# Sixteen blocks of 256 rows in place of interleaved rows, in a DMA-only ifftshift

## The chip, the cores and the metric

The kernel runs on one core of a Trainium2 chip. The metric is the time of one execution on the device in microseconds (us), as the median of several runs; lower is better. Besides the plain runs there is one profiled execution, whose trace records every instruction and every DMA packet.

## The reference

```python
def setup_inputs():
    return {"x": np.random.randn(8192, 8192).astype(np.float32)}

def reference(x):
    return np.fft.ifftshift(x)
```

With even sizes this swaps the four quadrants of the matrix: `out[r, c] = x[(r + 4096) % 8192, (c + 4096) % 8192]`. Nothing is computed; 268 MB are read and 268 MB written. A row of float32 has 32 KB, half a row 16 KB, and each half row of the output is one contiguous half row of the input.

## The kernel before

The kernel has no tile in on-chip memory and no compute instruction of its own. It is a list of DMAs that copy from the input to the output in the chip's main memory (HBM). Two instruction queues issue them in turn: SP's (`nc.sync`) writes the left half of the output rows (`h = 0`), from the right half of the input, and ACT's (`nc.scalar`) writes the right half (`h = hc`), from the left half of the input. In the profile SP's DMA queue is q1 and ACT's q10.

Each DMA is described by three dimensions, outermost first, as pairs of a step in elements and a count (line 26):

```python
dims = [[C, ENGINES], [ENGINES * C, per], [1, hc]]
```

The innermost is a contiguous half row of 16 KB. The outermost has 16 entries, one for each of the core's 16 DMA engines; here its step is one row (C = 8192 elements, 32 KB). The middle one has `per` = 32 entries with a step of 16 rows. So engine e copies the rows e, e + 16, e + 32 and so on of a group of 512 rows, and at any time the 16 engines work on neighbouring rows. A group's half is 8 MB. The loop of line 27 goes over the 16 groups; in each, line 29 takes SP's half and ACT's half. `src_row` (line 28) is the group's first row in the input.

There are 32 DMAs in all, 16 on each queue. The framework gives each one of eight semaphores in turn, four for each queue; before a semaphore is used again, the queue's issuing instruction waits for the DMA that had it, the one four before on that queue. Nothing else orders the DMAs. At the end SP waits until all have landed. The profile puts every DMA issue at line 30.

Of the kernel before, what the change touches and what calls it, by code (L numbers as in the profile page):

```python
# [1 line left out]

# [4 lines left out]


ENGINES = 16


@with_exitstack
def kernel(
    ctx: ExitStack,
    tc: tile.TileContext,
    x: bass.AP,
    out: bass.AP,
):
    nc = tc.nc
    R, C = x.shape  # L20
    hr = R // 2
    hc = C // 2


    per = 32
    dims = [[C, ENGINES], [ENGINES * C, per], [1, hc]]
    for row in range(0, R, ENGINES * per):
        src_row = (row + hr) % R
        for queue, h in ((nc.sync, 0), (nc.scalar, hc)):
            queue.dma_start(  # L30
                out=bass.AP(out.tensor, out.offset + row * C + h, dims),
                in_=bass.AP(x.tensor, x.offset + src_row * C + hc - h, dims),
            )


# [1 line left out]
_INS = ['x']  # L37
_OUTS = [((8192, 8192), 'float32')]


def kernel(**inputs):
    import numpy as _np
    import concourse.bacc as _bacc
    import concourse.tile as _tile
    from concourse import mybir as _mybir
    from concourse.bass_utils import run_bass_kernel_spmd as _run

    nc = _bacc.Bacc("TRN2", target_bir_lowering=False, num_devices=1)  # L48
    arrays, args = {}, []
    for name in _INS:  # L50
        a = _np.ascontiguousarray(inputs[name])
        if a.dtype.kind in "iu":
            a = a.astype(_np.int64)
        arrays[f"in_{name}_dram"] = a
        args.append(nc.dram_tensor(f"in_{name}_dram", a.shape, _mybir.dt.from_np(a.dtype), kind="ExternalInput").ap())
    for i, (shape, dtype) in enumerate(_OUTS):
        dt = _mybir.dt.from_np(_np.dtype(dtype))
        args.append(nc.dram_tensor(f"out_{i}_dram", shape, dt, kind="ExternalOutput").ap())
    with _tile.TileContext(nc) as tc:
        kernel(tc, *args)  # L60
    r = _run(nc, [arrays], core_ids=[0])
    got = tuple(r.results[0][f"out_{i}_dram"] for i in range(len(_OUTS)))
    return got[0]
```

## Time and profile before

| | us |
|---|---|
| median of 3 runs | 822.56 |
| lowest and highest | 821.65, 823.45 |
| the profiled execution | 822.98 |
| span of that execution, first to last instruction | 821.2 |
| from issue to landing of a DMA, median, ACT's queue | 204.1 |
| the same, SP's queue | 204.0 |

The profile's page shows the span in 40 equal slices of 20.5 us, with the mean busy share of the 16 DMA engines in tenths (9 is 90% or more) and the bytes that they moved, in GB/s; each byte copied is counted once there, though it is read and written. By the page, memory traffic in both directions together is 654 GB/s over the span. Below that, each DMA queue has its packets, its bytes and the time of its packets as a share of what 16 engines have. A packet here is one half row, or one small write to a semaphore at the end of a DMA's share on an engine. The only compute-engine instructions are four small fills of constants by the GpSimd engine, 0.2 us at the very start.

### The profile page before, as it was taken

The page shows a single profiled execution, that of the slowest core. Times are in us where ns is not written, and L with a number is a line of the kernel's source. Part 1 is how long each engine was busy: PE and PEld are TensorE (multiplying, and loading weights), DVE is VectorE, ACT ScalarE, POOL GpSimd, SP SyncE. Part 2 cuts the span into 40 slices and gives each one's busy share as a digit, 9 for nine tenths or more (in the row PEclk, how much of TensorE's full clock was granted, in tenths as well). Part 3 has the DMA queues.
Part 4 walks back from the last instruction along what each step waited for, and adds up shares of the span by engine and source line. Part 5 has one row for each costly group of instructions (what it writes and reads, how often), then busy time and mean ns, then how long its engine had stood idle before and what let it go on. Part 6 is the DMA issues. An engine that isn't in the chain of part 4 may idle for free. (4 is left out here: it accounts for less than half of the span.)

```text
span 821.2 us, 77 instructions
## 1 busy us (share of the span) xinstructions
POOL 0.2 (0%) x4
## 2 busy tenths in 40 slices
POOL 0000000000000000000000000000000000000000
DMA  8999999999999999999999999999999999999998
GB/s 296 333 324 329 331 328 334 330 330 329 327 330 329 331 326 332 332 327 328 330 330 330 330 323 330 324 330 330 332 326 329 330 322 333 329 329 327 330 329 276
DMA packets 16896, 268.44 MB, mean 327 GB/s; under 512 B 512, under 2 KB 512, under 8 KB 512
## 3 DMA queue, kind: packets, MB, share of 16 engines
q1 hardware_dynamic: 8448, 134.22, 50.2%
q10 hardware_dynamic: 8448, 134.22, 49.0%
HBM read 268.44 MB, written 268.44 MB: 654 GB/s over the span
## 5 line engine op out<-in xcount | busy, mean ns | idle before, releaser
L48 POOL MEMSET const-bfloat16-1.0<- 128x1 bf16 x1 | 0.1, 102 | 0.0
L48 POOL MEMSET const-uint8-127<- 128x1 uint8 x1 | 0.1, 102 | 0.0
L48 POOL MEMSET const-float32-0.0<- 128x1 f32 x1 | 0.1, 99 | 0.2 <-issue 0.2
L48 POOL MEMSET const-float32-1.0<- 128x1 f32 x1 | 0.1, 99 | 0.0
## 6 DMA issues: line engine op xcount, KB each, us to landing
out_dram<-in_x_dram ACTq DMA_DIRECT2D x16, 8192.0 KB, 204.1
out_dram<-in_x_dram SPq DMA_DIRECT2D x16, 8192.0 KB, 204.0
```

The source lines that it names most:

```text
L48: nc = _bacc.Bacc("TRN2", target_bir_lowering=False, num_devices=1)
```

## The change

The copy is cut into two halves of the output (rows 0 to 4095 and 4096 to 8191). In each half, an engine gets 256 neighbouring rows: the outermost step becomes `pitch` = 256 rows, 8 MB, and the middle step one row. Each half is copied in four parts of 64 rows an engine. A DMA has now 16 x 64 half rows, 16 MB, and there are 16 DMAs in all, 8 on each queue. SP and ACT keep their halves of the columns, and the issues still alternate. The last four lines are for pitches that leave rows over; with 256 none are left (16 x 256 = 4096) and they issue nothing.

```diff
-    per = 32
-    dims = [[C, ENGINES], [ENGINES * C, per], [1, hc]]
-    for row in range(0, R, ENGINES * per):
+    pitch = 256
+    parts = [64, 64, 64, 64]
+
+    def copy(queue, h, row, pitch, step, n):
+        dims = [[pitch * C, ENGINES], [step * C, n], [1, hc]]
         src_row = (row + hr) % R
-        for queue, h in ((nc.sync, 0), (nc.scalar, hc)):
-            queue.dma_start(
-                out=bass.AP(out.tensor, out.offset + row * C + h, dims),
-                in_=bass.AP(x.tensor, x.offset + src_row * C + hc - h, dims),
-            )
+        queue.dma_start(
+            out=bass.AP(out.tensor, out.offset + row * C + h, dims),
+            in_=bass.AP(x.tensor, x.offset + src_row * C + hc - h, dims),
+        )
+
+    for base in (0, hr):
+        row = base
+        for n in parts:
+            copy(nc.sync, 0, row, pitch, 1, n)
+            copy(nc.scalar, hc, row, pitch, 1, n)
+            row += n
+        rest = base + ENGINES * pitch
+        if rest < base + hr:
+            copy(nc.sync, 0, rest, 1, 1, 1)
+            copy(nc.scalar, hc, rest, 1, 1, 1)
```

## The prediction

> **What bounds the kernel now.** I read the page's slices first, then its queue table, then stretches of the start, then the waits of the issuing queue, and last the trace's single packet records.
>
> ```profile
> span 821.2 us, 77 instructions
> ...
> DMA  8999999999999999999999999999999999999998
> GB/s 296 333 324 329 331 328 334 330 330 329 327 330 329 331 326 332 332 327 328 330 330 330 330 323 330 324 330 330 332 326 329 330 322 333 329 329 327 330 329 276
> DMA packets 16896, 268.44 MB, mean 327 GB/s; under 512 B 512, under 2 KB 512, under 8 KB 512
> ## 3 DMA queue, kind: packets, MB, share of 16 engines
> q1 hardware_dynamic: 8448, 134.22, 50.2%
> q10 hardware_dynamic: 8448, 134.22, 49.0%
> ```
>
> No compute engine matters: the sixteen DMA engines are busy from end to end, at one flat rate. 16,384 packets carry a half row of 16 KB each (the other 512 are the small semaphore writes), so each engine carries 1,024. The mean packet follows: (0.502 + 0.490) x 821.2 us x 16 / 16,384 = 0.795 us, and the packet records give 795 ns too. 1,024 x 0.795 = 814.2 us; the 7.0 us left of the span are the head before the first packet (2.2 us), the last landing with the closing barrier (about 1.2 us after the last packet), and semaphore writes and small gaps. Around the span lie another 1.8 us (822.98 measured for this execution); the median of the runs is 0.4 us below that execution. So **the time is 1,024 times the mean packet**, plus 9.
>
> The mean hides two kinds of packet. By the records 32% take 608 to 611 ns, a hard floor (an engine at 26.8 GB/s), and the others spread up to 1,421 ns at the 99th percentile. A rate that every engine shared equally would put no packet at the floor; these look like chance collisions. The start shows what collides:
>
> ```profile
> 2.20:3.40 1.20, 0.00 (x0) 1.00 1.03 273
> 3.40:5.10 1.70, 0.00 (x0) 1.00 1.01 414
> 5.10:10.00 4.90, 0.00 (x0) 1.00 1.03 348
> 10.00:100.00 90.00, 0.00 (x0) 1.00 1.00 328
> ```
>
> The columns are the stretch, its length, the busy time of POOL, the clock, the DMA share and GB/s. From 2.2 us only SP's queue (q1) has packets; its first sixteen, which all begin within 0.6 us, average 1,090 ns, and the next 48 average 642 ns, almost the floor. At 5.1 us ACT's queue (q10) joins, and within 5 us the rate is 328 and stays there. Sixteen engines on sixteen neighbouring rows of one queue hardly disturb one another; engines on one queue disturb those on the other.
>
> ```profile
> SPq L30 <- DMA out_dram<-in_x_dram: 134.4, 12, 51.3
> ```
>
> These are SP's twelve waits for an earlier DMA to land before it reuses that DMA's semaphore. They cost nothing now: the three issues before already lie in the engines' queues (a DMA takes a median 204 us from issue to landing, four times the 51 us in which one passes).
>
> **The change, part by part.** *Work kept:* the same 16,384 half rows, 1,024 an engine, on the same two queues: no byte is added. *Instructions:* 32 DMAs become 16 of twice the size. That removes 256 semaphore writes, sixteen an engine, at 9 ns by the records: -0.14 us. The issues fall with them; they are hidden behind full queues except the first. It takes 0.65 us now by the trace's instruction record for 32 rows an engine; if the time goes with the rows, 64 rows take 1.3 us and everything begins 0.65 us later; if not, 0. I take 0.65. *Waits:* each queue still waits for its DMA four before; what is behind such a wait is only the next issue on that queue. Now the fourth issue takes 44 us, the first three 0.6 us each, so an engine's queue accepts 96 rows but not 128; with 64 a DMA the second issue will be the long one. Cover: at least 96 rows in each of two queues, 96 x 2 x 0.795 = 153 us. I cost it at 0; if the cover were gone, each wait would show about one first-round packet, 1.1 us, eight times in all, 9 us.
>
> *The order of addresses* is the real change. Now engine e is on row 16k + e: at any moment the sixteen engines of one queue are 32 KB apart, within 512 KB, and each hops 512 KB from packet to packet. Afterwards they are 8 MB apart, all at the same place inside their blocks, on the read and on the write side, and each goes forward by 32 KB. The trace has no row with that spacing, so the price is bounded. Best: every packet at the floor, 1,024 x (0.611 - 0.795) = -188 us. Worst: every packet like the 99th percentile, 1,024 x (1.421 - 0.795) = +641 us; the first round, in which all engines start at the same moment, is not far below (1,090 ns, +302 us). Between these I price collisions. Alone on one queue a packet costs 642 - 611 = 31 ns over the floor against 15 others, 2.1 ns each. With two queues about 7 of the others are on the packet's own queue and 8 on the other: 184 ns = 7 x 2.1 + 8 x p, p = 21 ns. What spares the own queue is, as I read it, the order: neighbouring rows at distinct places of memory. At 8 MB apart nothing spares them if memory folds 8 MB steps onto the same place, and all 15 others cost 21 ns: 611 + 15 x 21.2 = 929 ns. That is +134 ns a packet, +137 us. I take this value; half and double of the added 134 ns give 862 and 1,063 ns.
>
> The rule that speaks against the change: the Trainium skill, "DMA: Bandwidth & Descriptors", section "Latency and other measured facts", reports copies of 16 KiB pieces whose rate per direction falls with the row pitch, 207 GB/s at 512 KiB, 164 at 2 MiB, 103 at 4 and 8 MiB, and 214 with the pitch padded by 4 KiB. By its ratio of 214 to 103 the time here would be some 1,710 us, an estimate from that page. Its copies keep every stream of a tile inside the same 16 KiB window, while here each engine walks on through its whole block, so I don't take that figure; nothing in this trace shows the pitch.
>
> *Sum* on the profiled execution: 822.98 - 0.14 + 0.65 + 137 = 960.5, and 960 on the median's scale.
>
> **The rivals.**
>
> *Kept in step (slower by much).* All engines start together, and the arrivals of a DMA's sixteen semaphore writes lie 1.2 us apart for the first ACT DMA and only 2.5 us for the last of its kind at the end, so something holds the engines within three packets of one another. If that also holds them at the same place of sixteen folded blocks, every packet pays as in the worst rows: 1,024 x 1.09 to 1.421 us + 9.3, that is 1,125 to 1,464 us, and more is not excluded. Against: a packet that gets ahead finds memory free and should run away from the crowd. It decides from a mean packet over 1.09 us.
>
> *Steady streams (faster, the other side).* Engines spread out inside their blocks until each has its own place, and because all then move forward at one speed they stay clear of each other; an engine's two queues are then in the same few rows too, rather than several 512 KB hops apart. For it: 414 GB/s with one orderly queue, so memory can do it. Against: that order needs a spacing that nothing imposes, and the two queues remain. With all of the other queue's disturbance gone, 1,024 x 0.642 + 9.3 = 667 us; with half, (795 + 642) / 2 = 718 ns, 745 us. It decides as soon as the mean packet is below 795 ns.
>
> *A common limit (no change).* The flat 322 to 334 GB/s in 38 of 40 slices could be the total that memory gives for reads and writes mixed, whatever the order; then 823 us, within about 1%. Against: the 32% of packets at the floor, and 414 GB/s before 5.1 us.
>
> *The change doesn't do what it says.* No row names the engine of a packet; if the rows of a DMA were dealt out otherwise than block by block, an engine would hop over blocks. The small spread of landings fits equal shares either way. I fold this into the others.
>
> **How the numbers follow.** Collisions with all others: 0.44, 960 us, its own range 890 to 1,100 (1,024 x 0.862 and 1.063, + 9.3). Kept in step: 0.20, from 1,125 up. Steady streams: 0.26, 667 to 815. Common limit: 0.10, of which 0.04 within 0.2% of the median, 0.04 slower and 0.02 faster; about 0.2% is what a measurement of this kernel can tell from no change. Slower is 0.44 + 0.20 + 0.04 = 0.68, faster 0.26 + 0.02 = 0.28. The low end is 745 us, where half of the cross-queue cost is gone: about 0.10 lies below. The high end is 1,470, the 99th-percentile row kept throughout: about 0.08 lies above. The range is wide because the one cost that counts has no row of its own.
>
> **What would show it.** The mean packet, read from the queue table as above: 929 ns for the forecast, over 1,090 for kept in step, below 795 for steady streams. The stretch just after the first packets, while SP's queue is alone, tests the spacing by itself: now it is 414 GB/s; if 8 MB steps fold together it must be far lower, near 16 x 16 KB / 0.93 us = 282 GB/s or less, and if it is again about 414 my step is wrong, for then the own queue is still spared. If the rate starts low and rises over the first slices, the engines are escaping from the crowd. A spread of a DMA's landings well over 2.5 us would show that they have drifted apart. If SP's waits now leave gaps in the DMA's busy share, the cover was not what I took it for. The forecast is wrong in sign if the early stretch is slow but the later slices exceed 330 GB/s.

## The result: 2.12 times the time

The changed kernel takes 1,761 us (median of 4 runs, 1,733 to 1,794); the kernel before 823.0 us beside it. The ratio is 2.122, 95% interval 2.109 to 2.135. The forecast was slower, but 960 us, and the range ended at 1,470. The slow layouts vary by a few per cent from run to run, so the ratio takes the changed kernel's two runs within 1.5% of its fastest (1,733 and 1,757 us), and below its fastest run is given, as for every kernel that ran only twice; the others have their median.

The page of the profiled execution of the changed kernel (1,733.13 us), with the same lines as shown of before:

```profile
span 1731.3 us, 61 instructions
...
DMA  8999999999899999999989999999998999999999
GB/s 148 157 154 161 148 152 154 156 160 154 148 163 155 154 154 155 163 154 159 153 152 157 155 160 159 159 155 158 153 152 155 151 158 158 154 160 158 154 159 133
DMA packets 16640, 268.44 MB, mean 155 GB/s; under 512 B 256, under 2 KB 256, under 8 KB 256
## 3 DMA queue, kind: packets, MB, share of 16 engines
q1 hardware_dynamic: 8320, 134.22, 49.6%
q10 hardware_dynamic: 8320, 134.22, 49.0%
```

The DMA engines are as busy as before, at less than half the rate. The packets are the same 16,384 half rows, with 256 semaphore writes in place of 512. Each packet takes longer: (0.496 + 0.490) x 1,731.3 x 16 / 16,384 = 1.667 us, where it was 0.795, for the same 16 KB that the fastest packets of both traces move in 0.61. So a busy engine is here for the most part one that waits. The first stretches, the same as shown of before (stretch, length, POOL's busy time, clock, DMA share, GB/s):

```profile
2.20:3.40 1.20, 0.00 (x0) 1.00 1.10 191
3.40:5.10 1.70, 0.00 (x0) 1.00 1.04 241
5.10:10.00 4.90, 0.00 (x0) 1.00 0.90 134
10.00:100.00 90.00, 0.00 (x0) 1.00 0.94 156
```

By the packet records ACT's queue joins at 7.3 us here (5.1 us before). So SP's queue is alone when the rate is 241 GB/s against 414 before, and that is under the 282 that the prediction named as the sign that 8 MB steps fold together. Within a few microseconds the rate is at the 155 where it stays for the rest of the run: the loss is there from the first packets and nothing works it off.

### The profile page after: what moved, and what is told of

It is laid out like the page before. It is cut to its first block, busy times and chain, and to the rows that moved or that the text cites. A ratio compares the mean times of both kernels' runs of the same rounds, so it can differ in the third digit from the quotient of the medians.

```text
span 1731.3 us, 61 instructions
## 1 busy us (share of the span) xinstructions
POOL 0.2 (0%) x4
```

## The experiments

The rates are the page's means in the profiled execution, the mean packet and the spread are worked out from the trace's packet and semaphore records. Spread is the median time between the first and the last engine's landing of one DMA, in mean packets: it tells how closely the engines stay together. Not every run makes the whole output: e3 and e4 put the rows of each half in another order, and e5, e10, e12, e16 and e18 leave rows out (0.8% in e5, 3.1% in e12).

| run | us | GB/s | mean packet, us | spread, packets |
|---|---|---|---|---|
| before | 823 | 327 | 0.795 | 3.2 |
| changed | 1,733 | 155 | 1.667 | 2.2 |
| e1: 255 rows | 857 | 314 | 0.825 | 1.8 |
| e2: before, one queue | 825 | 326 | 0.797 | |
| e3: only reads far apart | 1,194 | 225 | 1.151 | |
| e4: only writes far apart | 1,313 | 205 | 1.264 | |
| e5: 8 MB + 4 KB | 1,420 | 188 | 1.379 | |
| e6: 8 engines | 1,251 | 210 | 0.623 | 4.2 |
| e7: 4 MB | 1,698 | 157 | 1.655 | 2.0 |
| e8: 1 MB | 813 | 331 | 0.787 | |
| e9: changed, one queue | 2,202 | 122 | 2.119 | 1.5 |
| e10: 12 engines | 788 | 252 | 0.727 | 146 |
| e11: 2 MB | 823 | 328 | 0.793 | 2.9 |
| e12: 8 MB + 16 KB | 992 | 255 | 1.020 | |
| e13: ACT 2 MB away | 2,285 | 113 | 2.267 | 1.6 |
| e14: ACT 4 MB away | 1,864 | 144 | 1.806 | |
| e15: 2 MB, one queue | 823 | 327 | 0.793 | |
| e16: 14 engines | 960 | 245 | 0.854 | 178 |
| e17: eight set back | 1,242 | 216 | 1.163 | |
| e18: before, 14 engines | 762 | 308 | 0.691 | 130 |

Beside e5 to e8 the kernel before took 812 us. In e6, e7, e10, e12, e13, e14 and e18 the profiled execution, which the last three columns come from, was the longer of the two (1,277, 1,716, 800, 1,021, 2,371, 1,871 and 763 us).

### Is it the spacing, or the way down the rows? (e1, e8)

```diff
-    pitch = 256
-    parts = [64, 64, 64, 64]
+    pitch = 255
+    parts = [64, 64, 64, 63]
```

> The changed kernel with one number different: blocks of 255 rows instead of 256 (the sixteen rows left over in each half go in one small DMA a queue). Engines still own neighbouring rows and go down them one by one, in DMAs of the same size; only the spacing of the engines falls from 8 MB to 8 MB less 32 KB. Theory A, the 8 MB spacing puts all engines at the same place of memory at the same time: the mean packet falls from 1.67 us to 0.61 to 0.85 us, time 640 to 880 us. Theory B, far-apart blocks walked row by row (or DMAs of twice the size) are what costs: it stays within 10% of the changed kernel, 1,600 to 1,800 us.

Measured: 857 us, 1.042 times the kernel before (1.038 to 1.046).

```profile
span 854.5 us, 65 instructions
...
GB/s 287 314 314 311 314 321 315 316 315 317 315 314 321 315 316 308 319 313 319 313 321 312 318 315 322 314 316 320 314 319 314 312 315 321 311 319 308 317 313 286
```

One row less between the engines doubles the rate of every slice. The stretch in which SP's queue is alone is back where it was before the change, in a run that differs in the spacing and the few rows left over:

```profile
3.40:5.10 1.70, 0.00 (x0) 1.00 1.00 414
```

The engines still own far-apart blocks, go down them row by row and use DMAs of twice the size, so none of these is the cause. The spacing is; that it puts the engines at the same place of memory, as theory A has it, is the reading of this and not yet shown. For e8 each engine took 32 neighbouring rows, in DMAs of the old size (shown against the kernel before, the rest of the loop left out):

```diff
-    per = 32
-    dims = [[C, ENGINES], [ENGINES * C, per], [1, hc]]
-    for row in range(0, R, ENGINES * per):
...
+    pitch, n = 32, 32
+    dims = [[pitch * C, ENGINES], [C, n], [1, hc]]
+    for base in range(0, R, ENGINES * pitch):
+        for row in range(base, base + pitch, n):
...
```

> Engines 1 MB apart (32 neighbouring rows each), with the 32 DMAs of the kernel before, 8 MB each: only which engine takes which row of a DMA differs from before. If blocks of neighbouring rows cost by themselves: over 1,300 us. If only large powers of two fold: between the kernel with 255 rows and the one before or slightly above, 820 to 1,000 us.

Measured: 813 us, ratio 1.001 (0.998 to 1.004). Blocks of neighbouring rows cost nothing by themselves.

### What the 0.184 us over the floor are (e2)

My price of a collision rested on the reading that the two queues disturb each other. This run has one queue.

```diff
-        for queue, h in ((nc.sync, 0), (nc.scalar, hc)):
+        for queue, h in ((nc.sync, 0), (nc.sync, hc)):
```

> The kernel before with all 32 DMAs on SP's queue, in the same order; ACT issues nothing. Theory C, the one behind my price of a collision (engines on one queue spare one another, the two queues disturb each other): the 414 GB/s of the first microseconds lasts, mean packet near 0.64 us, time 650 to 690 us. Theory D, the high early rate was only the start and the two-queue rate is what memory gives for this order: time 810 to 850 us.

Measured: 825 us, ratio 1.001 (0.999 to 1.003). Stretches of this run, columns as above:

```profile
2.20:3.40 1.20, 0.00 (x0) 1.00 1.21 300
3.40:5.10 1.70, 0.00 (x0) 1.00 0.93 395
5.10:10.00 4.90, 0.00 (x0) 1.00 1.03 351
10.00:100.00 90.00, 0.00 (x0) 1.00 0.99 323
```

The high early rate is there and fades in the same way, with no second queue to blame. Theory C is out: 414 GB/s was a property of the first microseconds.

### Reads or writes? (e3, e4)

```diff
+    near = [[C, ENGINES], [ENGINES * C, 64], [1, hc]]
+    far = [[256 * C, ENGINES], [C, 64], [1, hc]]
...
+                    out=bass.AP(out.tensor, out.offset + (base + ENGINES * i) * C + h, near),
+                    in_=bass.AP(x.tensor, x.offset + (src_base + i) * C + hc - h, far),
```

> The engines read blocks 8 MB apart as in the changed kernel, but write neighbouring rows as before; within each half the rows land in another order. If reads and writes pay alike for the 8 MB spacing: about half of the loss, some 1,200 to 1,400 us. If the side that is crowded sets the rate by itself: about 1,700 us. If reading does not pay: 800 to 900 us.

> The mirror image: the engines read neighbouring rows as before and write blocks 8 MB apart; within each half the rows land in another order. Alike: 1,200 to 1,400 us. Set by the crowded side: about 1,700 us. If writing does not pay: 800 to 900 us.

Measured: 1,194 us with far reads (this diff), 1,313 with far writes (the two lists and their row offsets exchanged). Over 823 that is 371 and 490 us, together 861 of the 910 to 938 lost. Both sides pay, the write side somewhat more.

### Which spacings? (e5, e7, e11, e12)

e7 and e11 give an engine 128 and 64 neighbouring rows: the edit of e8 with `pitch, n = 128, 64` and `64, 64`. e5 and e12 add to the spacing of the changed kernel:

```diff
-        dims = [[pitch * C, ENGINES], [step * C, n], [1, hc]]
+        dims = [[pitch * C + 1024, ENGINES], [step * C, n], [1, hc]]
```

(1,024 elements are 4 KB; e12 has 4,096. So that the blocks stay inside the matrix, the last part of each half is 62 rows in e5 and 56 in e12.)

> The changed kernel with the engines 8 MB + 4 KB apart in place of 8 MB, on both sides; each block has 254 rows (0.8% of the bytes are left out) and the cut between the halves of a row moves by 4 KB from engine to engine. Sixteen engines in step then stand over 64 KB of different places instead of one. If places of memory change every 4 KB or finer: 800 to 880 us. If they change by more than 16 KB, so that four or more engines still share one place: 1,000 to 1,400 us. If only whole rows count: about 1,700 us.

> Engines 4 MB apart (128 neighbouring rows each), DMAs of 16 x 64 half rows as in the changed kernel. If the folding is complete at 4 MB: 1,650 to 1,800 us. If the step from 4 to 8 MB still counts: 1,100 to 1,500 us.

> Engines 2 MB apart (64 neighbouring rows each, 16 + 16... here 8 DMAs a queue of 16 x 64 half rows). 1 MB cost nothing and 4 MB the whole loss. If the folding repeats at 4 MB, two places hold eight engines each here; if eight engines at a place are then as harmless as eight alone: 800 to 850 us. If every doubling of the spacing costs: 1,000 to 1,400 us.

> The changed kernel with engines 8 MB + 16 KB apart; each block has 248 rows (3.1% of the bytes are left out) and every other engine has the cut between the halves of a row moved by half a row. 0 KB of extra spacing gave 1,733 us, 4 KB 1,420 us, minus 32 KB 857 us. If the cost falls with the spread of the sixteen engines (64 KB at 4 KB, 256 KB here, 512 KB at 32 KB): 850 to 1,050 us. If less than a whole row of shift does not separate two engines that work packet by packet: 1,250 to 1,450 us.

Measured: 4 MB is as bad as 8 MB (1,698 us), 2 MB costs nothing (823 us, ratio 1.000, 0.998 to 1.003). Away from 8 MB the cost falls step by step with the extra spacing: 1,733 us at 0, 1,420 at 4 KB, 992 at 16 KB, 857 at 32 KB (less than 8 MB there, more in the other two). So the place that the engines share is not a row and not 4 KB: sixteen engines in step need several hundred KB between the first and the last (16 x 16 KB = 256 KB still costs, 16 x 32 KB = 512 KB hardly). Whether it is this whole stretch that counts or the 32 KB between neighbours, these runs can't tell.

### How many engines? (e6, e10, e16)

```diff
-ENGINES = 16
+ENGINES = 8
```

(e6 has this and the edit of e8 with `pitch, n = 256, 64`, and copies every row. e10 and e16 have 12 and 14 in the changed kernel, without its last four lines.)

> The changed kernel on eight engines instead of sixteen, still 8 MB apart (16 + 16 DMAs of 8 x 64 half rows; the other eight engines idle). Theory L, my linear price (each of the other engines at the same place costs a packet the same): (1,667 - 611) / 15 = 70 ns for each, 611 + 7 x 70 = 1,104 ns a packet, 2,048 packets an engine, 2,270 us. Theory S, one shared place that serves a fixed 155 GB/s however many ask: about 1,730 us, the time of sixteen engines, with a mean packet near 0.84 us. Floor of eight engines: 2,048 x 0.611 us = 1,251 us.

Measured: 1,251 us, neither of the two theories: it is the floor. The queues of this run, packets, MB and share of what 16 engines have:

```profile
q10 hardware_dynamic: 8320, 134.22, 25.2%
q1 hardware_dynamic: 8320, 134.22, 24.8%
```

Half the engines are busy, and 93% of the packets take the floor's 611 ns; the mean is 0.623. Eight engines 8 MB apart hardly feel one another, and move more (210 GB/s) than sixteen (155). My linear price would have had 1.104.

> The changed kernel on twelve engines; the last quarter of the rows of each half is left out, so each engine still has 1,024 packets and 201.3 MB are moved. Eight engines ran at the floor (mean packet 0.623 us, 210 GB/s), sixteen at 1.667 us (155 GB/s). If the folded place has a fixed limit of about 212 GB/s which sixteen engines only reach: 201.3 MB / 212 GB/s, about 950 us and a mean packet of 0.92 us. If the total falls as more engines crowd in: 180 GB/s or less, 1,120 to 1,300 us. If twelve still fit: 640 to 700 us.

> The changed kernel on fourteen engines; two of the sixteen blocks of each half are left out, 234.9 MB are moved, 1,024 packets an engine. Twelve engines moved 255 GB/s (788 us), sixteen 155. If the total falls smoothly: 200 to 215 GB/s, 1,100 to 1,180 us. If there is a sudden collapse at sixteen: 255 GB/s or more, 900 us or less.

Measured: 788 us for twelve, 960 for fourteen. The slices of these two pages, twelve engines first:

```profile
GB/s 163 228 272 275 277 273 280 244 206 247 263 268 278 280 243 231 248 239 271 274 251 254 254 268 276 241 258 263 282 292 239 262 271 282 275 217 217 216 215 192
```

```profile
GB/s 151 217 247 228 222 254 272 273 250 255 259 247 253 250 221 235 243 269 271 255 257 239 224 250 225 238 245 249 273 285 276 240 266 282 284 264 209 217 215 193
```

Both start low, rise within two or three slices and then swing between 206 and 292 GB/s until, in the last slices, eight engines are alone. The spread in the table says why: twelve and fourteen engines end a DMA 146 and 178 packets apart, sixteen 2.2 and eight 4.2. They do not scatter one by one. The landings of every DMA fall into groups: four and then eight with twelve engines (the eight 24 us later in the first DMA, 126 us at most), two, four and eight with fourteen, and in each the eight land within 3 us of one another. So these runs changed two things, the number and whether all engines stay in step, and the collapse between fourteen and sixteen can't be put down to the number alone.

### In step, or too many? (e9, e13, e14, e15, e17, e18)

Four runs asked which engines stand together. In the changed kernel ACT's queue is about 3.5 rows behind SP's by the packet records (the expectations say five to seven, which was too much).

```diff
-            copy(nc.scalar, hc, row, pitch, 1, n)
+            copy(nc.sync, hc, row, pitch, 1, n)
```

> The changed kernel with all 16 DMAs on SP's queue, in the same order. In the changed kernel ACT's queue runs some five to seven rows behind SP's, so the engines may stand in two crowds, one for each queue; on one queue there is a single crowd. If the size of a crowd at one place sets the rate: clearly slower than the changed kernel, 2,000 to 3,400 us. If what counts is that sixteen engines walk 8 MB apart with less than a few rows between them, whatever the queue: within 5% of the changed kernel, 1,650 to 1,850 us.

```diff
+            ahead = base + (row - base + 64) % pitch
             copy(nc.sync, 0, row, pitch, 1, n)
-            copy(nc.scalar, hc, row, pitch, 1, n)
+            copy(nc.scalar, hc, ahead, pitch, 1, n)
```

(This is e13; e14 has 128 in place of 64. e15 is e11 with both halves on `nc.sync`.)

> The changed kernel with ACT's four parts of each half in the order 2, 3, 4, 1, so that ACT's queue is 64 rows (2 MB) away from SP's instead of some five to seven rows. Engines, spacing, DMAs and bytes are the same; only which rows are worked on at the same time differs. Theory one crowd: the lag of a few rows does not separate the queues, sixteen engines stand at one place, and two places 2 MB apart with eight packets each relieve them: 820 to 1,200 us. Theory two crowds: the lag already separates them, eight packets at a place is what costs, and nothing changes: 1,650 to 1,850 us.

> The same with the order 3, 4, 1, 2: ACT is 128 rows (4 MB) away from SP, a distance that folds by the run with 4 MB. If 4 MB is the same place: as the changed kernel, 1,650 to 1,850 us, or up to 2,250 us (the time on one queue) if the few rows of lag did help. If the order of the parts helps by itself: below 1,500 us.

> Engines 2 MB apart with all DMAs on SP's queue: two folded places with eight engines each and no second queue. On two queues the same layout took 823 us. If eight packets at a place are what costs (two crowds): 1,500 us or more. If eight at a place are harmless on one queue too (one crowd): 800 to 900 us.

Measured: one queue is worse, 2,202 us. That fits the reading that the few rows between the queues help, but a second queue may help in another way too. ACT 4 MB away gives 1,864, near the changed kernel, as a fold at 4 MB would have it. But ACT 2 MB away gives 2,285, which neither theory had, while engines 2 MB apart on one queue take 823. One thing in the trace would fit the 2,285: the number of SP's packets in flight at one moment scatters more widely there (standard deviation 3.8 of some 16, 2.6 in the changed kernel), so that more engines stand on one side at once. That is argued, not tested, and in the kernel before, where nothing is lost, the same number is 3.2.

e17 delays eight of the engines and leaves the spacing alone:

```diff
+        if base == 0:
+            for first in (0, 8 * pitch):
+                copy(nc.sync, 0, first, pitch, 1, 32, 8)
+                copy(nc.scalar, hc, first, pitch, 1, 32, 8)
+            row += 32
```

(the last argument is the number of engines; the parts of the first half are then 64, 64, 64 and 32 rows).

> The changed kernel, but the first 32 rows of all sixteen blocks of the first half go in DMAs of eight engines (two for each queue), so engines 0 to 7 have 64 packets more on each queue to do than engines 8 to 15 before the common DMAs begin, and are behind them by 64 rows (2 MB) from then on if nothing brings them together. All rows are copied; engines 0 to 7 carry 1,088 packets and the others 960. Theory in step (the loss is sixteen engines at one place at one moment): two groups of eight at two places, mean packet 0.79 to 1.0 us on the slower engines, 880 to 1,150 us. Theory number of engines (sixteen streams 8 MB apart are too many whenever they are): 1,088 packets of 1.667 us, 1,800 us or more.

Measured: 1,242 us. Stretches of this run, columns as above:

```profile
10.00:160.00 150.00, 0.00 (x0) 1.00 1.00 194
160.00:600.00 440.00, 0.00 (x0) 1.00 1.00 221
600.00:1150.00 550.00, 0.00 (x0) 1.00 1.00 222
1160.00:1238.00 78.00, 0.00 (x0) 1.00 0.50 209
```

Once both groups are in the common DMAs, sixteen engines 8 MB apart move 221 GB/s, against 155 when they start together; in the last line the delayed eight finish alone. The landings show two groups: eight within 1 to 3 us, then nothing for some 147 us, then the other eight. That gap stays between 145 and 150 us for as long as both groups run: neither group catches up or runs away, so sixteen may stay together simply because they start together and are served alike. The moment matters, then, and not the number alone. Yet 221 is hardly more than eight engines alone (210), the time lies outside both ranges that I had written, and the rate is well below the 327 of the kernel before.

> The kernel before on fourteen engines, neighbouring rows 32 KB apart; 12.5% of the rows are left out, 234.9 MB, 1,024 packets an engine, as in the run with fourteen engines 8 MB apart (961 us). If engines out of step do not feel the spacing: within 5% of 961 us. If the 8 MB spacing still costs fourteen engines: 700 to 850 us. The spread of a DMA's landings shows whether fourteen engines drift apart here too (over 20 us) or only far apart.

```diff
-ENGINES = 16
+ENGINES = 14
...
-    for row in range(0, R, ENGINES * per):
+    for row in [base + i * ENGINES * per for base in (0, hr) for i in range(8)]:
```

Measured: 762 us, against 960 for fourteen engines 8 MB apart. The slices:

```profile
GB/s 290 325 323 320 330 326 324 327 330 325 318 330 324 326 326 331 331 325 329 330 326 333 321 318 322 309 330 306 330 323 311 324 288 333 319 222 215 215 218 183
```

Fourteen engines drift apart here too (130 packets, and again with eight of them together), so the drift comes with the number of engines, not with the spacing. With the groups out of step, the spacing still costs: about 246 GB/s far apart, 325 here. Of the two readings written down before the run the second holds: drift softens the loss and doesn't remove it. The same slices answer an older question: fourteen engines reach the 327 GB/s of sixteen. With one queue or two, with 32 KB, 1 MB or 2 MB between the engines, the rate is 326 to 331.

## Why the prediction was wrong, step by step

**The time is 1,024 times the mean packet:** right. 1,024 x 1.667 = 1,707 of a span of 1,731. The rest is 24 us where I had 7 for the span; away from the first and last 20 us the records show on average 15.86 packets in flight (15.97 before), so about 1% of the engines' time now lies idle, some 15 us.

**Instructions and waits:** the 256 semaphore writes less are there. The later start is not: the first issue still takes 0.65 us with 64 rows an engine, so my 0.65 us is 0. The engines' queues accepted two DMAs (128 rows) at once and stalled on the third, where I had the second as the long one. That the waits cost nothing holds: SP's list shows none before an issue any more.

```profile
SPq L71 <- DMA out_dram<-in_x_dram: 466.3, 2, 255.3
```

L71 is the end of the kernel; the waits for a landing before an issue have been swallowed by issues that now stall for about 210 us each on full queues.

**The order of addresses:** right in kind and sign, and the whole of the change. The term that failed is the added 134 ns a packet; it measured 1,667 - 795 = 872. It failed twice. First its input: I read the 184 ns over the floor as 8 x 21 ns of disturbance by the other queue. There is none (e2); 327 GB/s is a common limit that sixteen, and already fourteen, engines run into. The chance packets at the floor, which I took as proof against such a limit, don't exclude it. So 21 ns was the price of nothing and the 960 us had no ground; only the sign, which follows from the folding, held. Second its form: a fixed price for each neighbour. Eight engines pay 12 ns over the floor, sixteen 1,056 (e6 and the changed kernel).

**The rule of the Trainium skill that I set aside:** the row on HBM row pitch in "DMA: Bandwidth & Descriptors", section "Latency and other measured facts". Its ratio of 214 to 103 is 2.08; the measured one is 2.12, and that 4 and 8 MB are alike holds here too (1,698 and 1,733 us). I set it aside because each engine walks on through its whole block. The traces say that with sixteen engines this changes nothing, for none gets ahead: the spread is 2.2 packets after 1,024. In two points the measurements differ from that row and decide here: 2 MB costs nothing (823 us; the row has 164 of 214), and 4 KB of extra spacing brings back 313 of 910 us (1,420), not the full rate that the row gives for 4 KiB on a 4 MiB pitch. Its pitch is that of rows, mine that of engines, and no run here has its layout.

**The rivals:** kept in step was the one to choose. Its evidence was in my own prediction (landings 1.2 to 2.5 us apart), and e17 supports it: the same sixteen engines are 1.4 times as fast when eight are behind. What I held against it, that an engine ahead should run away, did not happen there either. Its price, from the slowest packets of the old trace, was still too low, because no row of that trace held such a crowd. Steady streams did not occur. The common limit is what bounds the kernel before, though it doesn't protect from a bad order, as that rival had it.

**What stays open:** why twelve and fourteen engines part into groups of eight, four and two, each in step, where sixteen do not part; why two groups 2 MB apart in time add so little (e17) and two queues 2 MB apart lose (e13), although engines 2 MB apart are free; and so whether the crowd's size at one place, as I used it, is the right picture. What it is in memory that folds at 4 MB was not tried. No run beats the kernel before on the full output: e2, e8, e11 and e15 are level with it.

## What to carry to other kernels

Before giving each DMA engine its own block of main memory, look at the distance between blocks. In this copy, with sixteen engines in step, 4 and 8 MB cost a factor of 2.1, 32 KB off 8 MB is enough to get nearly all of it back, and 32 KB, 1 MB and 2 MB were free. A DMA queue that is busy all the time says nothing about this; the mean packet of one layout against that of another does (1.667 and 0.795 us here, with the shortest at 0.608 in both). And when a price is needed that no row shows, a measured rule for nearly that pattern outweighs an argument for why it should not apply.

## What was not expected of the hardware

Eight engines 8 MB apart move 210 GB/s and sixteen 155. In DMAs on twelve or fourteen engines these part into groups of eight, four and two, 130 to 178 packets apart in the median; in DMAs on eight or sixteen all stay within six packets unless some are set back. A copy within main memory levels out at 326 to 331 GB/s each way on one core, with fourteen engines as with sixteen, whatever the queue and for every spacing from 32 KB to 2 MB that was tried.
